# A decoder layer on one Trainium2 core: weights of the out and down projections are loaded from the inputs into plain tiles and split from there

## The chip, the core and the metric

The kernel runs on one core of a Trainium2 chip. A core has a matrix engine (PE, TensorE, with its weight loads shown apart as PEld), a vector engine (DVE), a scalar engine (ACT), a general engine (POOL), a queue engine (SP) and 16 DMA engines that move data between DRAM and the on-chip memory. Each engine executes its own list of instructions in order, and waits on semaphores for the others. DMAs are issued by SP (queue q1), ACT (q10) and POOL (q0), each in its own order too: a DMA whose condition isn't met holds up whatever stands behind it in its issuer's list.

The metric is the device time of one execution in microseconds (us), lower is better. PE, DVE, ACT and POOL below are the names of the profile.

## The reference

One layer of a hybrid decoder on x of 2048 tokens by 1024 channels, in float32:

```python
h = rmsnorm(x, norm1)
z = h @ w_in                      # q, k, v | conv a, gate | lru gate, x
y = concat(attention(q, k, v),    # dilated sliding windows, 6 heads
           conv_module(a, gate),  # causal depthwise conv of 31 taps, LayerNorm, swish
           gelu(lru_gate) * rg_lru(conv4(lru_x)))
x = x + y @ w_out                                      # 1024 x 1024
x = x + relu(rmsnorm(x, norm2) @ w_up)**2 @ w_down     # 1024 x 4096, 4096 x 1024
return rmsnorm(x, final)
```

## The kernel before

**Split products.** Every large product is made of float32 operands that are split into a high half (a rounded copy, made on ACT by a CAST) and a low half (the rest, made on DVE by a subtraction). `halves(raw, h, l)` does both (L925 and L926; the copy of it for the in-projection is L242 and L243). A product then takes three matmuls: high by high, high by low, low by high. Up and down are besides done by a scheme of seven products of half blocks in place of eight.

**Stages.** The 2048 tokens are worked on in two halves h of 1024. The in-projection of half 0 fills about 0 to 257 us of the profiled span, that of half 1 about 257 to 500. Beside the second, the mixers of half 0 (attention, conv, LRU) run on DVE, ACT and POOL, with some small matmuls on PE. Then, for each half, come the out-projection (`outproj`, sixteen steps n, each of 24 matmuls into one of four banks), up (`up`) and down (`down`, 56 steps); half 0 takes about 500 to 1269 us, half 1 the rest. The mixers of half 1 lie in pieces beside up and down of half 0.

**What sets the order.** A scheduler puts each engine's instructions in order from the written program, its priorities and its own estimate of times. `issue_after` holds an instruction behind another, `high_priority` moves a group forward, and `sp_order` keeps the order in which the loads of `outproj` and `up` are written.

**Out and down weights.** Right behind the in-projection of half 0, ACT issues two DMAs from DRAM to DRAM: `out_w` is a copy of all of `w_out` (L1608), `down_w` of the left halves of the first sixteen row tiles of `w_down` (L1609), 4 MB each. `out_load(w)` (L953) loads one 128 by 1024 tile of `out_w` into the low tile of that weight's pair, and `out_split(w)` splits it in place; for w of 2 and 3 the pair is made of tiles of X. In `down`, block t of the weights is loaded by `t_load(t)` and split by `t_split(t)`. The first eight blocks (product 1) come from `down_w` into their own low tile (L1315) and are split in place, the later ones through the tiles `kept` and `second`.

**LRU of half 0** (`lru_mixer`). For each of three channel tiles a load `wide<-lscr` (L550, 513.5 KB, issued by SP) brings the projected x; DVE makes the four conv taps (L557, then L561 three times); ACT and DVE split the result (`wr<-wide`); PE makes the gates (L573 to L575). In the same stage PE works through the in-projection of half 1 (L262, L265, L268), whose results DVE takes out of the banks (`z<-mm`, L390 to L395) with the factor `row` of the norm (ACT L361, DVE L362).

**Change of halves.** Near the end of down of half 0 (`hooks(kp)`, and the lines behind `tail = down(...)`), the first steps of the next out-projection are put in front of the last work of `down`. That last work (`finish`) stores the output rows: DVE L1439 scales them in place, POOL L1443 stores them (`out<-v`, `out<-z`). The tiles of `low1` (`low_tiles(1)`) lie where `z1`, the last of these output tiles, was.

Of the kernel before, what the change touches and what calls it, by code (L numbers as in the profile page):

```python
# [12 lines left out]
P = 128  # L13
# [66 lines left out]
def body(tc, xt, w_in, w_v, w_out, w_up, w_down, vecs, lru_wa, lru_wx, consts, g_row, out, out_rows):  # L80
# [96 lines left out]
    gates_w = tc.dram_tile([3, P, 4 * P], F32, name="gates_w")  # L177
    out_w = tc.dram_tile([KT, P, HS], F32, name="out_w")
    cscr = tc.dram_tile([P, HS], F32, name="cscr")
    down_w = tc.dram_tile([2 * KT, P, NB], F32, name="down_w")  # L180

# [769 lines left out]

    def out_load(w, pairs):
        nc.sync.dma_start(f32(out_pair(w, pairs)[1]), out_w[CHANNELS[w]])  # L953

    def out_split(w, pairs):
        wh, wl = out_pair(w, pairs)
        halves(f32(wl), wh, wl)

# [10 lines left out]

    def out_first(pairs):  # L970
        out_load(0, pairs)
        out_load(1, pairs)
# [8 lines left out]
    def out_second(h, pairs):  # L981
        if not h:
            out_load(2, pairs)
            out_load(3, pairs)
        for n0, n1 in ((0, 2), (2, 4), (4, 5), (5, 8)):
            act_load(h, 0, n0, n1)

    def low_tiles(h):
        lp = pool(f"low{h}", 1, side="right", reuse_waits="tile")
        wraw = lp.tile([P, 4 * NB], F32, name="wraw")  # L990
        more = [lp.tile([P, HS], F32R, name=f"pair{5 + i}") for i in range(3)]
        plain = lp.tile([P, 3 * NB], F32, name="low")
        rest = [lp.tile([P, NB], F32, name=f"low{i}") for i in range(13)]
        at = [wraw[:, i * NB:(i + 1) * NB] for i in range(4)] + [plain[:, i * NB:(i + 1) * NB] for i in range(3)] + rest
        return wraw, plain, at, more

# [53 lines left out]

    def outproj(h, wts, banks, begun):
        at, pairs = wts.at, wts.pairs
# [44 lines left out]
        if not begun:  # L1097
            out_second(h, pairs)
        in_order = sp_order()
        residual(0)  # L1100
        residual(1)
        for n in range(16):
            if n >= begun:
                out_matmuls(n, pairs, banks, range(4))
                tick(OUT_SHARE)
                out_matmuls(n, pairs, banks, range(4, KT))
            w = {0: 1, 1: 2, 2: 3, 4: 6, 5: 7, 6: 4, 7: 5}.get(n, 0)
            if w > begun:
                out_split(w, pairs)
            if 1 <= n < 4:  # L1110
                for i in range(*((0, 3), (3, 6), (6, 8))[n - 1]):
                    act_split(0, i)
            if n == 12:
                for k in (2, 3):
                    split_op(S1, k, tiles[k][S1])
            with first():
                nc.vector.tensor_add(e_at[n % es], e_at[n % es], banks[n % 4])
            if 2 <= n < 6:
                out_load((6, 7, 4, 5)[n - 2], pairs)
            evac(n)  # L1120
            if n + 2 < 16:
                residual(n + 2)
            if n == 10:
                wts.load(0)
            elif n == 13:
                wts.sums(0)
                wts.first()
            elif n == 14:
                wts.second()
                wts.load_plain(0)  # L1130
            in_order()
            tick(OUT_SHARE)
# [151 lines left out]

    def down_steps(h):
        kept, second = [], []

        def t_tiles(t):
# [17 lines left out]
        def t_load(t):  # L1306
# [24 lines left out]
        def t_split(t):  # L1331
            n, kp = divmod(t, 8)
            th, tl = t_tiles(t)
            halves(f32(tl) if n == 0 else second[t % 3] if PRODUCTS[n] == 3 else kept[kp], th, tl)

        return s_load, s_split, s_tiles, t_load, t_sum, t_split, t_tiles, kept, second

    def down_prologue(steps):
        s_load, s_split, s_tiles, t_load, t_sum, t_split = steps[:6]

        def stage(i):
            if i == 0:
                s_load(0)
                t_load(2)
            elif i == 1:
                t_load(3)
            elif i == 2:
                t_load(0)
                t_load(4)
            elif i == 3:  # L1350
                s_load(1)
                t_load(5)
                t_split(2)
            elif i == 4:
                t_load(1)
                t_split(3)
            else:
                s_load(2)
                s_load(3)
                s_split(0)  # L1360
                t_split(0)
                s_split(1)
                t_split(1)

        return stage

    def down(h, steps, banks, hooks):
# [125 lines left out]

        upto = {"s load": 4, "s split": 2, "load": 6, "sum": 6, "split": 4}

# [110 lines left out]
    inproj(0)  # L1606
    with tc.issue_after(next(i for i in reversed(nc.cur_bb.bb.instructions) if i.engine == mybir.EngineType.Activation)):
        nc.scalar.dma_start(out_w, w_out)  # L1608
        nc.scalar.dma_start(down_w, w_down[0:2 * KT, :, 0:NB])  # L1609
    with tc.issue_after(last_x[0].ins):  # L1610
# [10 lines left out]
    def between(n):  # L1621
# [3 lines left out]
        elif n == len(COLUMN_ORDER[1]) - 2:  # L1625
            close("wide")
            pairs.extend(left_pairs(0))
            out_first(pairs)

    inproj(1, between)  # L1630
    close("pmain", "z", "plain")
    aside[0] = mixers(1)
# [6 lines left out]
    for h in range(2):  # L1639
        wraw, plain, at, more = low_tiles(h)  # L1640
        pairs = pairs + more
        wts = Weights(wraw, plain, at, pairs)
        rest = outproj(h, wts, banks, begun)
        steps = down_steps(h)
        up(h, wts, banks, rest, down_prologue(steps))
# [4 lines left out]
        def hooks(kp):  # L1650
# [3 lines left out]
            elif h == 0 and kp == 1:  # L1654
# [3 lines left out]
                state_["pairs"] = left_pairs(1)  # L1658
            elif h == 0 and kp == 2:
                out_load(0, state_["pairs"])  # L1660
            elif h == 0:
                for n0, n1 in ((), ((0, 2),), ((2, 4),), ((4, 5), (5, 6)), ((6, 8),), ())[kp - 2]:
                    act_load(1, 1, n0, n1)
                if kp in (3, 5, 6):
                    out_load({3: 1, 5: 2, 6: 3}[kp], state_["pairs"])
                if kp > 3:
                    act_split(1, 2 * kp - 8)
                    act_split(1, 2 * kp - 7)
                if kp == 5:
                    out_split(0, state_["pairs"])  # L1670

        tail = down(h, steps, banks, hooks)
        close(f"second{h}")
        if h:
            while chores:
                chore()
            run(tail)
            close("early1", "late1")
        else:
            pairs = state_["pairs"]  # L1680
            out_matmuls(0, pairs, banks, range(KT))
            out_second(1, pairs)
            while chores:
# [6 lines left out]
            run(tail)  # L1690
            close("late0")
            begun = 2
# [45 lines left out]
```

## Time and profile before

| | before |
|---|---|
| median of 3 runs | 1989.8 us (1986.52 to 1991.84) |
| profiled execution, its own time | 1988.35 us |
| its span, first to last instruction | 1986.5 us |
| mean granted TensorE clock | 0.994 |
| DVE busy | 1448.0 us (73%) |
| ACT busy | 1054.4 us (53%) |
| POOL busy | 168.2 us (8%) |
| moved by DMA | 399.78 MB: q1 342.02, q0 45.38, q10 10.76 |
| DRAM read, written | 287.47 MB, 119.00 MB |

The same span by stage:

| stretch, us | PE busy | DVE busy | ACT busy | PE clock |
|---|---|---|---|---|
| 0 to 257 (257) | 245.81 | 225.99 | 146.53 | 1.00 |
| 257 to 500 (243) | 223.18 | 161.10 | 101.59 | 0.96 |
| 500 to 1269 (769) | 762.34 | 596.57 | 462.71 | 1.00 |
| 1269 to 1986.5 (717.5) | 707.36 | 464.30 | 343.56 | 1.00 |

What PE is not busy is the difference of the first number in a row's brackets and its PE time: 11.2, 19.8, 6.7 and 10.1 us. The last column is the clock that the throttle granted to PE, 1.00 being full speed; a busy PE at a low clock loses time that doesn't show as idle.

### The profile page before, as it was taken

Reading aid. Unit: us, or ns where it says so; the run is one execution under the profiler, and the core shown is the slowest. Engines: PE = TensorE matmul, PEld = TensorE weight load, DVE = VectorE, ACT = ScalarE, POOL = GpSimd, SP = SyncE. Lnnn points to the kernel's source line nnn. Section 1 sums busy time; section 2 is a strip of 40 time slices with the busy share of each in tenths; the row PEclk is TensorE's granted clock in tenths of the full one; section 3 lists DMA queues with packets and bytes.
Section 4 is the critical chain, followed back from the end, with each engine's and each line's share of the span. In section 5 each row is a group of like instructions: output and inputs, shape, how many; then the busy total and the mean of one; then the engine's idle time right before and its main releaser. Section 6 shows DMA issues by size and latency. Waiting matters only on the chain.

```text
span 1986.5 us, 25512 instructions
## 1 busy us (share of the span) xinstructions
PE 1938.7 (98%) x8906; PEld 1590.3 (80%) x8906; DVE 1448.0 (73%) x1976; ACT 1054.4 (53%) x1637; POOL 168.2 (8%) x297
## 2 busy tenths in 40 slices
PE   7999979999999999999999999999999999999998
PEld 6887757779787787888888888788888887888886
DVE  7899766784568665878878899867555555577884
ACT  6145946513558764555565566346555545444343
POOL 0024100000023413000000000100000000000001
PEclk9999989999999999999999999999999999999999
DMA  5556586635556647445788687764444447786773
GB/s 170 159 160 184 161 281 200 208 125 160 184 173 185 207 149 234 169 151 179 272 292 293 225 287 248 249 194 146 149 148 149 154 148 259 240 285 212 264 260 138
DMA packets 202124, 399.78 MB, mean 201 GB/s; under 512 B 25382, under 2 KB 33814, under 8 KB 201932
## 3 DMA queue, kind: packets, MB, share of 16 engines
q1 hardware_dynamic: 182548, 342.02, 51.2%
q0 software_dynamic: 16096, 45.38, 7.9%
q10 hardware_dynamic: 3352, 10.76, 1.6%
q8 instruction: 70, 1.15, 0.2%
q14 instruction: 58, 0.48, 0.1%
HBM read 287.47 MB, written 119.00 MB: 205 GB/s over the span
## 4 chain that ended last, share of the span: by engine, by line
PE 70%; DVE 12%; DMA 9%; ACT 5%; issue 4%; SPq 0%; POOL 0%; DVEq 0%; ACTq 0%; POOLq 0%
PE bank L1153 9%; PE bank L1154 9%; PE bank L1155 9%; PE bank L1517 7%; PE bank L1515 7%; PE bank L1516 7%; PE mm L262 3%; PE mm L268 3%; PE mm L265 3%; PE bank L966 2%; PE bank L967 2%; PE bank L968 2%; DVE wide L474 2%; DMA second<-in_w_down 2%; DVE rounded L926 1%
## 5 line engine op out<-in xcount | busy, mean ns | idle before, releaser
L1153 PE MATMUL bank<-rounded,pair 128*128 128x512 f32 x896 | 351.2, 392 | 2.7 <-ACT low L1162 2.0
L1154 PE MATMUL bank<-rounded,pair 128*128 128x512 f32 x896 | 351.0, 392 | 0.0
L1155 PE MATMUL bank<-rounded,pair 128*128 128x512 f32 x896 | 350.9, 392 | 0.0
L1515 PE MATMUL bank<-rounded,rounded 128*128 128x512 f32 x688 | 268.1, 390 | 1.6 <-DVE z L1528 0.8
L1517 PE MATMUL bank<-rounded,rounded 128*128 128x512 f32 x688 | 268.0, 389 | 1.4 <-DVE rounded L926 1.4
L1516 PE MATMUL bank<-rounded,rounded 128*128 128x512 f32 x688 | 267.7, 389 | 0.0
L926 DVE TENSOR_TENSOR rounded<-rounded 128x1024 fp32r<-128x1024 f32 (+1 forms) x172 | 186.9, 1098 | 73.0 <-ACT rounded L925 72.6
L925 ACT CAST rounded<-rounded 128x1024 fp32r<-128x1024 f32 (+1 forms) x172 | 161.1, 949 | 132.2 <-DMA rounded<-fscr 92.1
L1153 PEld LDWEIGHTS bank<-rounded,pair 128*128 128x128 f32 x896 | 168.4, 188 | 40.1 <-ACT low L1162 2.4
L1155 PEld LDWEIGHTS bank<-rounded,pair 128*128 128x128 f32 x896 | 168.2, 188 | 36.0 <-issue 0.2
L1154 PEld LDWEIGHTS bank<-rounded,pair 128*128 128x128 f32 x896 | 168.2, 188 | 35.4 <-issue 0.2
L262 PE MATMUL mm<-rounded,rounded 128*128 128x512 f32 x496 | 159.7, 398 | 8.5 <-ACT rounded L242 6.6
L265 PE MATMUL mm<-rounded,rounded 128*128 128x512 f32 x496 | 158.6, 396 | 0.0
L268 PE MATMUL mm<-rounded,rounded 128*128 128x512 f32 x496 | 157.8, 395 | 0.0
L925 ACT CAST rounded<-kept 128x1024 fp32r<-128x1024 f32 x80 | 84.0, 1050 | 136.8 <-DVE kept L1325 67.0
L1515 PEld LDWEIGHTS bank<-rounded,rounded 128*128 128x128 f32 x688 | 129.1, 188 | 29.5 <-DVE z L1528 1.3
L1517 PEld LDWEIGHTS bank<-rounded,rounded 128*128 128x128 f32 x688 | 129.2, 188 | 29.1 <-DVE rounded L926 2.3
L1516 PEld LDWEIGHTS bank<-rounded,rounded 128*128 128x128 f32 x688 | 129.2, 188 | 27.0
L242 ACT CAST rounded<-raw 128x512 fp32r<-128x512 f32 (+1 forms) x96 | 55.7, 583 | 145.1 <-PE mm L265 91.1
L925 ACT CAST pair<-wraw 128x1024 fp32r<-128x1024 f32 x64 | 67.1, 1048 | 112.6 <-PE bank L1154 108.3
L926 DVE TENSOR_TENSOR rounded<-kept,rounded 128x1024 fp32r<-128x1024 f32 x80 | 97.8, 1223 | 38.4 <-ACT rounded L925 38.1
L926 DVE TENSOR_TENSOR pair<-wraw,pair 128x1024 fp32r<-128x1024 f32 x64 | 78.2, 1222 | 61.6 <-ACT pair L925 61.5
(375 smaller groups left out, 3680.3 us busy)
## 6 DMA issues: line engine op xcount, KB each, us to landing
fscr<-low SPq DMA_DIRECT2D x224, 256.0 KB, 2.1
rounded<-fscr SPq DMA_DIRECT2D x112, 512.0 KB, 3.9
second<-in_w_down SPq DMA_DIRECT2D x80, 512.0 KB, 5.4
kept<-in_w_down SPq DMA_DIRECT2D x48, 512.0 KB, 5.3
raw<-in_w_in SPq DMA_DIRECT2D x64, 256.0 KB, 3.9
low<-in_w_up SPq DMA_DIRECT2D x64, 256.0 KB, 3.1
wraw<-in_w_up SPq DMA_DIRECT2D x64, 256.0 KB, 2.9
raw<-in_xt SPq DMA_DIRECT2D x32, 256.0 KB, 3.4
```

Source lines behind the costliest of these rows:

```text
L242: nc.scalar.copy(h, raw)
L262: nc.tensor.matmul(bank, wh[:, sl], ah[:, cols], start=first_, stop=False)
L265: nc.tensor.matmul(bank, wh[:, sl], al[:, cols], start=False, stop=False)
L268: nc.tensor.matmul(bank, wl[:, sl], ah[:, cols], start=False, stop=last_)
L925: nc.scalar.copy(h, raw)
L926: nc.vector.tensor_sub(l, raw, f32(h))
L1153: nc.tensor.matmul(bank, wh[:, sl], hi(x), start=fresh and k == 0, stop=False, **kw)
L1154: nc.tensor.matmul(bank, wh[:, sl], lo(x), start=False, stop=False, **kw)
L1155: nc.tensor.matmul(bank, wl[:, sl], hi(x), start=False, stop=k == KH - 1, **kw)
L1515: nc.tensor.matmul(banks[j], th[:, c], sh[:, x], start=fresh and k0, stop=False, **kw)
L1516: nc.tensor.matmul(banks[j], th[:, c], sl[:, x], start=False, stop=False, **kw)
L1517: nc.tensor.matmul(banks[j], tl[:, c], sh[:, x], start=False, stop=k1, **kw)
```

## The change

The two DRAM copies and their tensors are gone. `out_load(w, tile_)` loads from `w_out` into a plain tile that it is given, and `out_split` splits from that tile into the pair. `t_load` loads the blocks of product 1 from `w_down`, the first six into three `two` tiles, the others into `second`. The lines that are left out give the plain tiles: a new pool `stage` of two tiles for w of 0 and 1 in half 0, and in `low_tiles` five tiles `two` of twice the width in place of ten single ones.

```diff
-    out_w = tc.dram_tile([KT, P, HS], F32, name="out_w")
-    down_w = tc.dram_tile([2 * KT, P, NB], F32, name="down_w")
...
-    def out_load(w, pairs):
-        nc.sync.dma_start(f32(out_pair(w, pairs)[1]), out_w[CHANNELS[w]])
+    plain_w = {}
+
+    def out_load(w, tile_):
+        plain_w[w] = tile_
+        nc.sync.dma_start(tile_, w_out[CHANNELS[w]])
 
     def out_split(w, pairs):
         wh, wl = out_pair(w, pairs)
-        halves(f32(wl), wh, wl)
+        halves(plain_w.pop(w), wh, wl)
...
         if not begun:
-            out_second(h, pairs)
+            out_second(h, twos)
+        else:
+            out_load(3, twos[1])
...
             if 2 <= n < 6:
-                out_load((6, 7, 4, 5)[n - 2], pairs)
+                out_load((6, 7, 4, 5)[n - 2], twos[n % 2])
...
+        plain_t = {t: twos[i] for t, i in ((2, 0), (3, 1), (0, 2), (4, 0), (5, 1), (1, 2))}
...
             if i == 1:
-                nc.sync.dma_start(two(f32(t_tiles(t)[1])), down_w[2 * kp:2 * kp + 2].rearrange("k p n -> p k n"))
+                block(plain_t[t] if t in plain_t else second[t % 3], 0, 0)
...
-        upto = {"s load": 4, "s split": 2, "load": 6, "sum": 6, "split": 4}
+        upto = {"s load": 4, "s split": 2, "load": 6, "sum": 6, "split": 6}
...
-    with tc.issue_after(next(i for i in reversed(nc.cur_bb.bb.instructions) if i.engine == mybir.EngineType.Activation)):
-        nc.scalar.dma_start(out_w, w_out)
-        nc.scalar.dma_start(down_w, w_down[0:2 * KT, :, 0:NB])
...
-            elif h == 0 and kp == 2:
-                out_load(0, state_["pairs"])
...
-                if kp in (3, 5, 6):
-                    out_load({3: 1, 5: 2, 6: 3}[kp], state_["pairs"])
...
+                for n0, n1 in {6: ((2, 4),), 7: ((4, 5), (5, 8))}.get(kp, ()):
+                    act_load(1, 0, n0, n1)
+                if 3 <= kp < 6:
+                    out_load(kp - 3, steps[8][(kp - 1) % 3])
...
-            out_second(1, pairs)
+            act_load(1, 0, 0, 2)
```

For half 1 the loads of w of 0, 1 and 2 go into the tiles `second` at kp of 3, 4 and 5, and that of w of 3 is written at the head of `outproj(1)`, into `two1`. In the prologue of down, each of the first six blocks is loaded a stage earlier and all six are split there, where before it was four.

The scheduler then moves other work as well. **The first LRU tile of half 0.** These are ACT's rows of before behind the in-projection of half 0; DMAs in ACT's list are issued there, and `x2` marks two like rows:

```order
L404 ACTIVATE z<-z 128x1024 [waits DVE_49]
L1608 DMA out_w<-in_w_out 64x16384 [waits DMAHW4_49]
L1609 DMA down_w<-in_w_down 2048x512 [waits DMAHW6_49]
L361 ACT_TABLE_LOAD
L361 ACTIVATE row_105<-mm,eps_r 128x512 [waits PE_49] x2
```

After the change the same place of ACT's list reads (line numbers are two lower here):

```order
L402 ACTIVATE z<-z 128x1024 [waits DVE_49]
L502 ACT_TABLE_LOAD
L502 ACTIVATE wide<-cb,eps_l 128x512 [waits PE_49]
L240 CAST rounded_83<-raw_99 128x512 [waits DMAHW3_49,PE_49,Activation_49]
L781 COPY m<-mb 128x128
```

The copies are gone, and a square root of the conv mixer (L502, L504 of before) stands ahead of the factor of the norm. On DVE this is what stood between the statistics of the attention (L755, L760) and the taps of the LRU (L557, which waits for the load `wide<-lscr`):

```order
L755 ISA m,stat_142<-mb,m 128x128 [waits PE_49]
L760 TENSOR_SCALAR ncol_144<-stat_142 128x2 [waits DVE_49]
L557 TENSOR_SCALAR wide<-wide,vec 128x1024 [waits DMAHW3_49]
L561 SCALAR_TENSOR_TENSOR wide<-wide,vec 128x1024 [waits DVE_49] x3
L362 RECIPROCAL row_105<-row_105 128x512 [waits Activation_49] x2
L393 TENSOR_TENSOR z<-mm,row_105 128x512 [waits DVE_49,PE_49] x2
```

And this is what stands there now (the taps are L555 and L559):

```order
L758 TENSOR_SCALAR ncol_142<-stat_140 128x2 [waits DVE_49]
L503 RECIPROCAL wide<-wide 128x512 [waits Activation_49]
L241 TENSOR_TENSOR rounded_83<-raw_99,rounded_83 128x512 [waits DMAHW3_49,PE_49,Activation_49]
L753 ISA m,stat_140<-mb,m 128x128 [waits PE_49]
L506 TENSOR_TENSOR wide<-wide 128x512 [waits DVE_49]
L555 TENSOR_SCALAR wide<-wide,vec 128x1024 [waits DMAHW3_49]
L559 SCALAR_TENSOR_TENSOR wide<-wide,vec 128x1024 [waits DVE_49] x3
L360 RECIPROCAL row_105<-row_105 128x512 [waits Activation_49] x2
L391 TENSOR_TENSOR z<-mm,row_105 128x512 [waits DVE_49,PE_49] x2
```

Work of the conv and the attention now precedes the taps in DVE's list.

**The change of halves.** SP's rows of before, at the first steps of `outproj(1)`; `m<-in_xt` loads the residual, `xscr` and `ascr` are scratch, `pair_9839` and `pair_9841` are the low tiles of w of 6 and 7:

```order
L1066 DMA m<-in_xt 128x512 [waits DMAHW0_49,DMASW7_49]
L1066 DMA m<-in_xt 128x512 [waits DMASW7_49,DMAHW1_49,DMASW6_49,DMASW2_49]
L1074 DMA xscr<-m 128x512 [waits DMAHW2_49,DVE_49]
L1066 DMA m<-in_xt 128x512 [waits DMAHW3_49,DMASW7_49]
L1074 DMA xscr<-m 128x512 [waits DMAHW4_49,DVE_49]
L1081 DMA ascr<-wraw 128x512 [waits DMAHW5_49,Activation_49]
L1066 DMA m<-in_xt 128x512 [waits DMAHW6_49]
L953 DMA pair_9839<-out_w 128x1024 [waits DMAHW7_49]
```

SP's rows now, from the same residual on; the first `two_9840` is w of 3, `two_9839` is w of 6, and DMASW1 to DMASW4 are semaphores of stores that POOL issues:

```order
L1069 DMA m<-in_xt 128x512 [waits DMAHW5_49,DMASW7_49]
L1069 DMA m<-in_xt 128x512 [waits DMASW7_49,DMAHW6_49,DMASW6_49,DMASW2_49]
L1077 DMA xscr<-m 128x512 [waits DMAHW7_49,DVE_49]
L1069 DMA m<-in_xt 128x512 [waits DMAHW0_49,DMASW7_49]
L1077 DMA xscr<-m 128x512 [waits DMAHW1_49,DVE_49]
L954 DMA two_9840<-in_w_out 128x1024 [waits DMASW3_49,DMASW4_49,DMASW2_49,DMAHW2_49,DMASW1_49,DVE_49]
L1084 DMA ascr<-wraw 128x512 [waits DMAHW3_49,Activation_49]
L1069 DMA m<-in_xt 128x512 [waits DMAHW4_49]
L954 DMA two_9839<-in_w_out 128x1024 [waits DMAHW5_49]
```

The load of w of 3 now stands here, and waits for the last four stores of `z1`, over which `two1` lies. On PE, before, the second step that uses `rounded7` (the pair of w of 2 and 3; bank 4011) followed right upon the first (bank 4014):

```order
L967 MATMUL bank_4014<-rounded_80,rounded_9486 128x512
L968 MATMUL bank_4014<-rounded_80,rounded_9486 128x512
L966 MATMUL bank_4011<-rounded_79,rounded_9486 128x512
L967 MATMUL bank_4011<-rounded_79,rounded_9486 128x512
L968 MATMUL bank_4011<-rounded_79,rounded_9486 128x512
```

Now a whole step on `pair0` (bank 4016, 24 matmuls) and nine matmuls of the next (bank 4017) lie between; its last rows, and the first of the second `rounded7` step (bank 4015):

```order
L969 MATMUL bank_4016<-rounded_82,pair_9488 128x512
L967 MATMUL bank_4017<-rounded_81,pair_9489 128x512 [waits DVE_49]
L968 MATMUL bank_4017<-rounded_81,pair_9489 128x512
L969 MATMUL bank_4017<-rounded_81,pair_9490 128x512
L967 MATMUL bank_4015<-rounded_79,rounded_9483 128x512 [waits Activation_49]
L968 MATMUL bank_4015<-rounded_79,rounded_9483 128x512
```

The wait for ACT in that row is for the CAST of w of 3 from `two1`.

More of the change, by code (lines that the diff above doesn't have):

```diff
@@ L968, in out_matmuls, with out_first @@
             nc.tensor.matmul(bank, wl[:, sl], hi(b0 + k), start=False, stop=k == KT - 1)
-    def out_first(pairs):
-        out_load(0, pairs)
-        out_load(1, pairs)
+    def out_first(pairs, tiles):
+        out_load(0, tiles[0])
+        out_load(1, tiles[1])
         for n0, n1 in ((0, 2), (2, 4), (4, 5), (5, 8)):
@@ L979, in out_first, with out_second @@
                 act_split(1, n)
[L981 to L984, printed above, removed]
+            out_split(1, pairs)
+    def out_second(h, tiles):
+        out_load(2, tiles[0])
+        out_load(3, tiles[1])
         for n0, n1 in ((0, 2), (2, 4), (4, 5), (5, 8)):
@@ L992, in low_tiles @@
         plain = lp.tile([P, 3 * NB], F32, name="low")
-        rest = [lp.tile([P, NB], F32, name=f"low{i}") for i in range(13)]
-        at = [wraw[:, i * NB:(i + 1) * NB] for i in range(4)] + [plain[:, i * NB:(i + 1) * NB] for i in range(3)] + rest
-        return wraw, plain, at, more
+        twos = [lp.tile([P, HS], F32, name=f"two{i}") for i in range(5)]
+        ones = [lp.tile([P, NB], F32, name=f"low{i}") for i in range(3)]
+        both = [t[:, i * NB:(i + 1) * NB] for t in twos for i in range(2)]
+        at = [wraw[:, i * NB:(i + 1) * NB] for i in range(4)] + [plain[:, i * NB:(i + 1) * NB] for i in range(3)]
+        return wraw, plain, at + ones[:1] + both[:4] + ones[1:] + both[4:], more, twos
     class Weights:
@@ L1049, in sp_order, with outproj @@
         return in_order
-    def outproj(h, wts, banks, begun):
+    def outproj(h, wts, banks, begun, twos):
         at, pairs = wts.at, wts.pairs
@@ L1106, in outproj @@
                 out_matmuls(n, pairs, banks, range(4, KT))
-            w = {0: 1, 1: 2, 2: 3, 4: 6, 5: 7, 6: 4, 7: 5}.get(n, 0)
-            if w > begun:
+            w = {1: 2, 2: 3, 4: 6, 5: 7, 6: 4, 7: 5}.get(n)
+            if w in plain_w:
                 out_split(w, pairs)
@@ L1283, in up, with down_steps @@
             done = (a21, a22, a11, a12)
-    def down_steps(h):
+    def down_steps(h, twos):
         kept, second = [], []
+        plain_t = {t: twos[i] for t, i in ((2, 0), (3, 1), (0, 2), (4, 0), (5, 1), (1, 2))}
         def t_tiles(t):
@@ L1333, in t_split @@
             th, tl = t_tiles(t)
-            halves(f32(tl) if n == 0 else second[t % 3] if PRODUCTS[n] == 3 else kept[kp], th, tl)
+            halves(plain_t[t] if t in plain_t else second[t % 3] if n == 0 or PRODUCTS[n] == 3 else kept[kp], th, tl)
         return s_load, s_split, s_tiles, t_load, t_sum, t_split, t_tiles, kept, second
@@ L1344, in stage @@
                 t_load(2)
+                t_load(3)
             elif i == 1:
-                t_load(3)
+                t_load(0)
             elif i == 2:
-                t_load(0)
+                t_split(2)
                 t_load(4)
@@ L1351, in stage @@
                 s_load(1)
+                t_split(3)
                 t_load(5)
-                t_split(2)
             elif i == 4:
+                t_split(0)
                 t_load(1)
-                t_split(3)
+                t_split(4)
             else:
@@ L1360, in stage @@
                 s_split(0)
-                t_split(0)
                 s_split(1)
                 t_split(1)
+                t_split(5)
         return stage
@@ L1627, in between @@
             pairs.extend(left_pairs(0))
-            out_first(pairs)
+            stage = pool("stage", 1, reuse_waits="tile")
+            out_first(pairs, [stage.tile([P, HS], F32, name=f"stage{i}") for i in range(2)])
     inproj(1, between)
-    close("pmain", "z", "plain")
+    close("pmain", "z", "plain", "stage")
     aside[0] = mixers(1)
@@ L1639, in body @@
     for h in range(2):
-        wraw, plain, at, more = low_tiles(h)
+        wraw, plain, at, more, twos = low_tiles(h)
         pairs = pairs + more
         wts = Weights(wraw, plain, at, pairs)
-        rest = outproj(h, wts, banks, begun)
-        steps = down_steps(h)
+        rest = outproj(h, wts, banks, begun, twos)
+        steps = down_steps(h, twos[2:])
         up(h, wts, banks, rest, down_prologue(steps))
@@ L1670, in hooks @@
                     out_split(0, state_["pairs"])
+                for n0, n1 in {6: ((2, 4),), 7: ((4, 5), (5, 8))}.get(kp, ()):
+                    act_load(1, 0, n0, n1)
+                if 3 <= kp < 6:
+                    out_load(kp - 3, steps[8][(kp - 1) % 3])
         tail = down(h, steps, banks, hooks)
-        close(f"second{h}")
         if h:
@@ L1677, in body @@
             run(tail)
-            close("early1", "late1")
+            close("second1", "early1", "late1")
         else:
@@ L1690, in body @@
             run(tail)
-            close("late0")
+            close("second0", "late0")
             begun = 2
```

## The prediction

> **What bounds the kernel now.** I start with the page: busy time of the engines, then the forty slices of the span (49.7 us each).
>
> ```profile
> PE 1938.7 (98%) x8906; PEld 1590.3 (80%) x8906; DVE 1448.0 (73%) x1976; ACT 1054.4 (53%) x1637; POOL 168.2 (8%) x297
> ...
> PE   7999979999999999999999999999999999999998
> ...
> PEclk9999989999999999999999999999999999999999
> DMA  5556586635556647445788687764444447786773
> ```
>
> PE is busy for 1938.7 of 1986.5 us, so all idle time of PE together is 47.8 us, and no rearrangement of loads can win more than that and what a low clock costs. Three slices show idle time: the start, the end, and slice 6 (248 to 298 us). Slice 6 is also the one with a low clock and the one of the busiest DMA engines in the first half of the span. The change removes two DMAs that are issued just there, so the next view is the table by windows, with the waits of 255 to 345 us (columns: total, times, longest).
>
> ```profile
> 250.00:300.00 50.00, 35.59 (x145) 27.26 (x144) 30.65 (x42) 21.97 (x38) 0.00 (x0) 0.85 0.86 281
> 300.00:350.00 50.00, 48.80 (x214) 38.81 (x212) 31.03 (x52) 32.62 (x43) 1.79 (x3) 0.98 0.65 199
> ...
> DVE wide L557 <- DMA wide<-lscr: 22.5, 2, 18.3
> ...
> PE cb L573 <- ACT wr L242: 10.1, 1, 10.1
> ACT wr L242 <- DVE wide L561: 10.0, 2, 9.8
> ...
> PE mb L753 <- DVE stat L755: 3.3, 1, 3.3
> ```
>
> PE lacks 50 - 35.59 = 14.4 us in the first window and 1.2 in the second. Read from the bottom up the waits are one chain: PE waits 10.1 us for the split of the LRU input, ACT waits for the taps, DVE waits 18.3 us for the load `wide<-lscr`. The timeline (start, duration, engine, and idle time before it in brackets) and the chain of waits give the times:
>
> ```profile
> 258.73 0.63 ACTq L1608 DMA_DIRECT2D out_w<-in_w_out  x1
> 260.40 0.50 ACTq L1609 DMA_DIRECT2D down_w<-in_w_down  x1
> ...
> 260.31 0.42 SPq L550 DMA_DIRECT2D wide<-lscr  x1
> ...
> 281.80 0.81 DVE L557 TENSOR_SCALAR wide<-wide,vec 128x1024 f32<-128x1024 f32 x1 [18.30 <-DMA wide<-lscr]
> ...
> 287.33 0.80 PE L573 MATMUL cb<-wr 128*128 128x512 f32 x1 [10.05 <-ACT wr L242]
> ...
> 296.25 0.80 PE L753 MATMUL mb<-mr 128*128 128x256 f32 x2 [3.28 <-DVE stat L755]
> ```
>
> ```profile
> 260.31 21.47 DMA wide<-lscr
> ...
> 323.19 4.39 DMA wide<-lscr
> ```
>
> The copies are issued at 258.7 and 260.4; the load that is issued beside them takes 21.5 us, the same load at 323.2 takes 4.4. That is the contention: 17 us of delay on DVE, which executes in order and so can't do the reciprocals (L362) and the evacuations behind it either. PE runs dry twice, for 10.05 and for 3.28 us. Behind both the clock is low:
>
> ```profile
> 285.00:290.00 5.00, 2.67 (x6) 2.15 (x7) 4.96 (x4) 1.18 (x2) 0.00 (x0) 0.50 1.04 329
> 290.00:295.00 5.00, 2.97 (x10) 2.01 (x8) 5.00 (x5) 2.13 (x3) 0.00 (x0) 0.84 0.27 102
> 295.00:300.00 5.00, 3.75 (x11) 3.17 (x12) 5.00 (x8) 0.71 (x3) 0.00 (x0) 0.50 0.70 221
> 300.00:305.00 5.00, 5.00 (x20) 4.05 (x19) 2.46 (x5) 2.44 (x3) 0.00 (x0) 0.83 0.02 4
> ```
>
> Busy time by what the clock lacks: 2.67 x 0.50 + 2.97 x 0.16 = 1.8 us behind the first wait, 3.75 x 0.50 + 5.00 x 0.17 = 2.7 behind the second.
>
> [...]
>
> **First term: the stall at 260 to 302 us.** It costs 14.4 + 1.2 us idle and 1.8 + 2.7 us of low clock, 20.1 together. Not all of it goes. In the new order ACT makes the root of the conv mixer ahead of the factor of the norm (`row`), each with a table load of its own, and PE's next matmuls use the bank that the factor is read from.
>
> ```profile
> 272.70 1.28 ACT L766 ACT_TABLE_LOAD   x1
> ```
>
> I replayed the new order of PE, ACT and DVE by hand with the durations of the trace. PE then waits 2.2 us near 273 for the factor (two table loads of 1.28 us, less what lies beside other work), and up to 1 us at each of two later gates of the LRU; there is no wait at the first. The 1.2 us of the second window I leave in. 20.1 - 2.2 - 2 - 1.2 = **14.7 us gained**. The bounds: at least the wait of 10.05 us and the clock behind it without those 2.2 (10.05 + 1.8 - 2.2 = 9.6), at most all but the 1.2 (18.9). From 302 us on PE is nearly always busy, so what is won there is kept unless something else ends last; the next such place is at 430 to 450 us:
>
> ```profile
> 430.00:450.00 20.00, 17.45 (x80) 15.55 (x79) 13.46 (x16) 3.68 (x7) 0.00 (x0) 0.91 0.52 176
> ...
> PE mm L425 <- DVE z L393: 2.5, 1, 2.5
> ```
>
> There PE lacks 2.55 us and about 17.45 x 0.09 = 1.6 us of clock, by an evacuation that stands late in DVE's list. DVE arrives earlier and has fewer taps ahead of it now; I take **1 us gained**, between -1 (the order gets a little worse) and 4.1 (all of it).
>
> **Second term: the change of halves.** The load of w of 3 now waits for the last stores of `z1`, in SP's list, and PE has 24 + 9 matmuls to do before it needs the result. The rows of before at this place, from the timeline of POOL, ACT, SP and DVE, a window of 2 us, and one piece of the chain of waits:
>
> ```profile
> 1285.54 2.14 POOL L1443 DMA_DIRECT2D out<-z  x4
> ...
> 1297.02 0.72 ACT L1073 ACTIVATE low<-m,vec 128x512 f32<-128x512 f32 x1 [4.54 <-DMA out<-z]
> ...
> 1285.52 0.87 SPq L953 DMA_DIRECT2D pair<-out_w  x1
> ...
> 1289.91 0.66 SPq L953 DMA_DIRECT2D pair<-out_w  x1
> ...
> 1287.24 0.69 DVE L1117 TENSOR_TENSOR m<-m,bank 128x512 f32<-128x512 f32 x1 [0.40 <-PE bank L968]
> ...
> 1291.00:1293.00 2.00, 2.00 (x11) 1.65 (x10) 0.49 (x1) 0.64 (x1) 0.00 (x0) 1.00 1.03 415
> ...
> 1276.31 0.23 PE bank L966
> ```
>
> The median landing times of like DMAs, from the table of DMA issues (the last number), and the cast and the subtraction of such a tile (mean ns of one behind the bar):
>
> ```profile
> out<-z POOLq DMA_DIRECT2D x20, 256.0 KB, 6.4
> ...
> out<-v POOLq DMA_DIRECT2D x4, 256.0 KB, 2.8
> ...
> second<-in_w_down SPq DMA_DIRECT2D x80, 512.0 KB, 5.4
> ...
> rounded<-down_w SPq DMA_DIRECT2D x16, 512.0 KB, 5.8
> ...
> rounded<-fscr SPq DMA_DIRECT2D x112, 512.0 KB, 3.9
> ...
> L925 ACT CAST rounded<-kept 128x1024 fp32r<-128x1024 f32 x80 | 84.0, 1050 | 136.8 <-DVE kept L1325 67.0
> ...
> L926 DVE TENSOR_TENSOR rounded<-kept,rounded 128x1024 fp32r<-128x1024 f32 x80 | 97.8, 1223 | 38.4 <-ACT rounded L925 38.1
> ```
>
> PE ends the step before at about 1287.1 (DVE takes its bank at 1287.24). 33 matmuls of 0.23 us cover it to 1294.7. The last of the four stores is issued at about 1287.15. In before they had landed by 1297.0, while two loads of 512 KB ran beside them and the DMA engines were full (share 1.03). Of these two loads the first is now the one that waits, so I take the stores' median, 6.4 us: landed at 1293.5. The load, 5.4 us, ends at 1298.9, the cast, 1.05 us, at 1300.0. PE waits 5.3 us, and loses some 2.5 us of clock behind it (1.8 and 2.7 above): **7.8 us lost**. The bounds: stores in 2.8 us and load in 3.9 give 1295.0, a wait of 0.3 and no loss to speak of; stores at 1297.0 as before and load in 5.8 give 1303.9, a wait of 9.2 and 2.7 of clock, 11.9 lost. Behind the waiting load on SP stand `ascr`, the residual `m` and the load of w of 6. They are needed one step later or more (the residual by an evacuation whose bank comes up again only after three further steps, 3 x 24 x 0.23 = 16.6 us), so they cost nothing as long as the wait stays under some 12 us. The weights of 6, 7, 4 and 5 then pass through two tiles by turns: per tile 5.4 + 1.05 us and a subtraction of 1.22, against 11 us of matmuls (48 x 0.23) for each weight.
>
> **The rest at nothing.** As many splits, and loads of the same size; the 8 MB that the copies read and wrote are gone. Two casts and two subtractions of down's prologue come earlier. The waits there that they could lengthen or shorten are small:
>
> ```profile
> PE bank L1517 <- DVE rounded L926: 1.4, 2, 0.9
> ```
>
> I bound this at 2 us either way; if ACT and DVE had no idle time in the prologue, the four would cost 2 x 1.05 + 2 x 1.2 = 4.5 us once per half.
>
> **Sum.** Profiled execution 1988.35 - 14.7 - 1 + 7.8 = **1980.5 us**. The median of the runs is 1.45 us above the profiled one, 1989.8, so this is 0.4 to 0.5% faster. About 0.3%, or 6 us, is what a measurement of this kernel can tell from no change: faster is below 1983.8, slower above 1995.8.
>
> [...]
>
> **The rivals.**
> 1. *The stores are early.* The full DMA engines of before were due to the loads beside the stores, and one of them now waits. Then the wait of PE is 0 to 1 us: 1988.35 - 14.7 - 1 + 0.5 = 1973. For it: share 1.03 at 1291; against it: the stores' median is 6.4 us over all twenty.
> 2. *The stores are as late as before.* 11.9 us lost: 1988.35 - 14.7 - 1 + 11.9 = 1984.6; with the smallest first term, 9.6, it is 1989.7, no change. For it: ACT really waited until 1297.02.
> 3. *The first stall only changes its name (slower).* In DVE's new list, statistics, a reciprocal and multiplies of conv and attention stand ahead of the taps, each waiting for PE or ACT. If one of them holds DVE until about 281.8, as the load did, the first term is 0 and only the second is left: 1988.35 + 7.8 = 1996.2. It decides for slower when less than about 0.5 us of the first term is won. Against it: ACT and PE have their inputs by 276 in the replay, and `wide<-lscr` at 4.4 us would land at 265.
> 4. *The copies weren't the cause*, and the load takes its 21.5 us from traffic of its own queue; the change then doesn't do what it says in this stage. The time is that of 3, but the wait would still read `wide<-lscr`. The 4.4 us of the second load speak against it.
>
> **How the numbers follow.** Forecast (1977 to 1985) 0.45; stores early (below 1977) 0.25; stores late (1985 to 1991) 0.18; 3 and 4 together 0.12, a third of it with enough of the first term left to be no change. Faster by over 0.3%: most of the forecast and all of the first rival, 0.67; within 0.3%: the end of the forecast, the second rival and that third, 0.24; slower 0.09. The likeliest case gives the time, 1980.5. The range leaves out the best ends of both terms and the slower cases: 1970 to 1990.
>
> **What would show it.** In the profile after: slice 6 of PE at 9 with PEclk 9; `wide<-lscr` near 4 to 5 us and no long wait at the taps; PE's wait for the gates gone. A new wait of PE near 1280 us on ACT's cast `rounded<-two`, 5 us long, with SP waiting for `out<-z` at the load of w of 3, and a clock of about 0.5 for some 5 us behind it. PE idle outside these two places within 2 us of before. Wrong would be: DVE waiting 10 us or more ahead of the taps (rival 3), a load of over 15 us there (rival 4), or PE's idle time growing in down or up, which no term here covers.

## The result: 1.0% faster, and outside the predicted range

| | before | after |
|---|---|---|
| median | 1988.63 us (4 runs, 1986.52 to 1991.84) | 1967.61 us (4 runs, 1966.72 to 1970.98) |
| ratio of after to before | | 0.9896, 95% interval 0.9877 to 0.9915 |
| profiled execution, its own time | 1988.35 us | 1968.2 us |
| its span | 1986.5 us | 1966.4 us |

1980.5 was forecast, with a range of 1970 to 1990. The direction was right; the gain, 20 us, is two and a half times the 8 that were forecast.

**The profile after.** The page's busy times and slices (a slice is 49.2 us here):

```profile
PE 1933.0 (98%) x8906; PEld 1585.9 (81%) x8906; DVE 1448.0 (74%) x1976; ACT 1050.9 (53%) x1635; POOL 168.4 (9%) x297
...
PE   8999999999999999999999999999999999999998
...
PEclk9999999999999999999999999999999999999999
DMA  5556557444666657445787696755444436686773
```

Slice 6 of PE has gone from 7 to 9, and its clock from 8 to 9. PE's idle time fell from 47.8 to 1966.4 - 1933.0 = 33.4 us, by 14.4. The same 8906 matmuls kept PE busy 1938.7 us before and 1933.0 now: those 5.7 us were low clock. Together this is the 20.1 us of the spans.

Where they were won, the same stretches of the program show, in before and in after. A stretch begins or ends with a certain matmul: the first of the out-projection of half 0 (508.1 and 487.8 us), the last gate of the LRU (1202.5, 1180.8), the last `pair` step of the out-projection of half 1 (1357.4, 1338.7), the last of down's product with two `rounded` tiles (1928.9, 1908.3). Columns: stretch, its length, busy times, clock, DMA share, GB/s. Before:

```profile
257.00:508.10 251.10, 231.28 (x1034) 191.57 (x1034) 165.61 (x214) 104.31 (x146) 8.70 (x15) 0.96 0.59 190
508.10:1202.50 694.40, 688.04 (x3218) 560.64 (x3218) 534.73 (x769) 421.55 (x659) 95.42 (x165) 1.00 0.66 218
1202.50:1357.40 154.90, 153.98 (x675) 126.03 (x674) 121.33 (x155) 79.31 (x114) 9.94 (x18) 1.00 0.65 212
1357.40:1928.90 571.50, 569.77 (x2502) 469.09 (x2501) 369.60 (x402) 281.78 (x377) 0.00 (x0) 1.00 0.58 203
```

After:

```profile
257.00:487.80 230.80, 224.84 (x1036) 186.63 (x1035) 165.92 (x216) 101.80 (x145) 8.72 (x15) 1.00 0.54 169
487.80:1180.80 693.00, 688.74 (x3218) 561.79 (x3218) 535.70 (x770) 421.01 (x658) 95.51 (x165) 1.00 0.66 219
1180.80:1338.70 157.90, 155.04 (x675) 125.79 (x674) 121.83 (x155) 80.74 (x116) 9.94 (x18) 1.00 0.64 208
1338.70:1908.30 569.60, 569.35 (x2501) 468.99 (x2500) 369.26 (x402) 281.58 (x377) 0.00 (x0) 1.00 0.59 204
```

The stage of the mixers is 251.1 - 230.8 = 20.3 us shorter (13.9 idle, 6.4 busy at a higher clock). Up and down of half 0 win 1.4, the change of halves loses 3.0, half 1 wins 1.9, and the rest, 57.6 against 58.1 us, loses 0.5: 20.1.

**The stage of the mixers after**, by windows, by waits and by the DMA issues of 257 to 282 us:

```profile
250.00:300.00 50.00, 46.81 (x216) 36.34 (x215) 40.09 (x66) 41.05 (x65) 0.60 (x1) 1.00 0.64 194
300.00:350.00 50.00, 47.23 (x201) 36.76 (x200) 39.29 (x48) 28.86 (x35) 3.08 (x6) 1.00 0.73 233
...
430.00:450.00 20.00, 20.00 (x117) 19.98 (x116) 7.31 (x14) 5.25 (x10) 4.83 (x8) 1.00 0.66 183
```

```profile
DVE wide L555 <- DMA wide<-lscr: 2.7, 2, 1.6
...
PE mm L260 <- ACT row L359: 2.3, 1, 2.3
...
PE cb L571 <- ACT wr L240: 1.3, 1, 1.3
```

```profile
wide<-lscr SPq DMA_DIRECT2D x1, 513.5 KB, 6.2
```

The load takes 6.2 us in place of 21.5, DVE's wait for it is at most 1.6 in place of 18.3, and PE's wait for the first gate is gone. PE's wait of 2.3 us for the factor of the norm stands where the replay had 2.2. What is idle there, 3.2 + 2.8 us, is close to the 5.4 that the prediction left in. The stall at 430 to 450 us has gone altogether.

**The change of halves after**, by the timelines of DVE, POOL, SP, ACT and PE:

```profile
1265.37 0.69 DVE L1122 TENSOR_TENSOR m<-m,bank 128x512 f32<-128x512 f32 x1 [0.42 <-PE bank L969]
...
1263.65 2.21 POOL L1451 DMA_DIRECT2D out<-z  x4
...
1269.46 0.33 SPq L954 DMA_DIRECT2D two<-in_w_out  x1
...
1269.43 0.72 ACT L1076 ACTIVATE low<-m,vec 128x512 f32<-128x512 f32 x1 [2.97 <-DMA out<-z]
...
1274.00 1.04 ACT L923 CAST rounded<-two 128x1024 fp32r<-128x1024 f32 x1 [3.34 <-DMA two<-in_w_out]
...
1275.10 0.50 PE L967 MATMUL bank<-rounded,rounded 128*128 128x512 f32 x1 [2.28 <-ACT rounded L923]
```

The chain is the one that was forecast: stores, load, cast, matmul. PE came to the place at 1275.10 - 2.28 = 1272.8, which is 1265.2 and 33 matmuls of 0.23 us. But the last store was issued at about 1265.3 and all had landed by 1269.4, 4.1 us later and not 6.4; the load was in by 1274.0, 4.5 us and not 5.4. While these stores were under way SP issued nothing (1261.3 to 1269.5 us), where before it issued six DMAs at 1284.3 to 1289.9; that this made the stores faster is read from the traces and wasn't tried apart. So PE waits 2.3 us, and its clock stays at 1.00 behind it.

### The profile page after: what moved, and what is told of

It is laid out like the page before. It is cut to its first block, busy times and chain, and to the rows that moved or that the text cites. A ratio compares the mean times of both kernels' runs of the same rounds, so it can differ in the third digit from the quotient of the medians.

```text
span 1966.4 us, 25491 instructions
## 1 busy us (share of the span) xinstructions
PE 1933.0 (98%) x8906; PEld 1585.9 (81%) x8906; DVE 1448.0 (74%) x1976; ACT 1050.9 (53%) x1635; POOL 168.4 (9%) x297
## 4 chain that ended last, share of the span: by engine, by line
PE 82%; DMA 6%; DVE 6%; ACT 3%; issue 2%; POOL 0%; SPq 0%; DVEq 0%; ACTq 0%; POOLq 0%
PE bank L1158 10%; PE bank L1159 10%; PE bank L1160 10%; PE bank L1523 9%; PE bank L1525 9%; PE bank L1524 9%; PE mm L260 4%; PE mm L263 4%; PE mm L266 4%; PE bank L969 2%; PE bank L967 2%; PE bank L968 2%; DMA raw<-in_xt 1%; PE mm L423 1%; PE mm L425 1%
## 5 line engine op out<-in xcount | busy, mean ns | idle before, releaser
L924 DVE TENSOR_TENSOR rounded<-rounded 128x1024 fp32r<-128x1024 f32 (+1 forms) x152 | 162.4, 1080 | 62.5 <-ACT rounded L923 62.1
L923 ACT CAST rounded<-rounded 128x1024 fp32r<-128x1024 f32 (+1 forms) x152 | 139.9, 935 | 112.4 <-DMA rounded<-fscr 89.0
L260 PE MATMUL mm<-rounded,rounded 128*128 128x512 f32 x496 | 158.3, 395 | 10.4 <-ACT rounded L240 7.0
L266 PE MATMUL mm<-rounded,rounded 128*128 128x512 f32 x496 | 156.4, 392 | 0.0
L263 PE MATMUL mm<-rounded,rounded 128*128 128x512 f32 x496 | 156.3, 393 | 0.0
```

What stands on the lines that cost most here:

```text
L260: nc.tensor.matmul(bank, wh[:, sl], ah[:, cols], start=first_, stop=False)
L263: nc.tensor.matmul(bank, wh[:, sl], al[:, cols], start=False, stop=False)
L266: nc.tensor.matmul(bank, wl[:, sl], ah[:, cols], start=False, stop=last_)
L923: nc.scalar.copy(h, raw)
L924: nc.vector.tensor_sub(l, raw, f32(h))
```

## The experiments

All ratios are to runs of the kernel before on the same chip, taken beside them. "Load" is the first `wide<-lscr`; "start" is the time of the first matmul of the out-projection of half 0 in the profiled execution. That one execution can lie off the median: by 7.6 us in out_rows, 3.7 in down_only, 3.0 in before_rows (all slower than their medians), and at most 2.1 in the others of this table.

| kernel | copies | load, us | start, us | median, us | ratio, 95% interval |
|---|---|---|---|---|---|
| before | 4 MB in 64 KB pieces, 4 MB in 2 KB | 21.5 | 508.1 | 1988.63 | 1 |
| after | none | 6.2 | 487.8 | 1967.61 | 0.9896 (0.9877 to 0.9915) |
| both_copies | as before, unused | 21.0 | 505.2 | 1987.16 | 0.9995 (0.9977 to 1.0012) |
| half_copies | 4 MB in 64 KB pieces | 18.4 | 506.1 | 1985.39 | 0.9979 (0.9956 to 1.0003) |
| out_rows | 4 MB in 4 KB pieces | 13.0 | 500.8 | 1977.70 | 0.9946 (0.9930 to 0.9961) |
| down_only | 4 MB in 2 KB pieces | 10.5 | 500.5 | 1981.94 | 0.9966 (0.9948 to 0.9985) |
| before_rows | 4 MB in 4 KB pieces, 4 MB in 2 KB | 12.2 | 501.9 | 1983.67 | 0.9976 (0.9964 to 0.9989) |
| sliver | 0.5 MB in 32 KB pieces | 6.4 | 492.4 | 1970.40 | 0.9915 (0.9890 to 0.9939) |

**The copies put back, without use (both_copies).**

```diff
...
     inproj(0)
+    with tc.issue_after(next(i for i in reversed(nc.cur_bb.bb.instructions) if i.engine == mybir.EngineType.Activation)):
+        nc.scalar.dma_start(out_w, w_out)
+        nc.scalar.dma_start(down_w, w_down[0:2 * KT, :, 0:NB])
```

> The changed kernel with the two DRAM copies put back where they were (nothing reads them); weights still come straight from the inputs. With a DMA issued at that place the scheduler falls back to the order of before for the mixers of half 0. Theory A (the traffic of the copies is the cause): the load of the LRU input takes about 21 us again, PE lacks some 14 us at 260 to 300 us, and the time is 1987 to 1990 us. Theory B (the new data path of the weights, fewer or earlier loads, won the time): the time stays at 1968 to 1971.

All of the gain is gone: 1987.16 us, not to be told from before. The load takes 21.0 us, and PE lacks 13.5 us at 250 to 300 us:

```profile
250.00:300.00 50.00, 36.54 (x147) 28.29 (x146) 30.08 (x40) 21.20 (x36) 0.00 (x0) 0.86 0.83 277
```

The new data path of the weights by itself, with its changed loads, tiles and splits, wins nothing that can be measured (the interval leaves it 0.23% at most). Theory B falls.

**A sixteenth of the bytes, in the same order (sliver).** With a DMA at that place, here of 0.5 MB, the scheduler chooses the order of before for the mixers; this run has that order and hardly any traffic. The traces of both_copies, sliver, half_copies, out_rows and down_only list the same instructions in the same order on every engine, so these five differ in their copies alone. The edit, against both_copies:

```diff
-        nc.scalar.dma_start(out_w, w_out)
-        nc.scalar.dma_start(down_w, w_down[0:2 * KT, :, 0:NB])
+        nc.scalar.dma_start(out_w[0:1], w_out[0:1])
```

> As the one with both copies, but only a sixteenth of their bytes is copied (512 KB of 8 MB), at the same place. The orders of PE, DVE and SP are those of the kernel with both copies. Theory A1 (traffic alone): the load of the LRU input takes 4 to 7 us, and the time is 1968 to 1971. Theory A2 (the order of the mixers that comes with a DMA at this place, not the bytes): 1985 to 1990. Between them, the part above 1968 is what the order costs.

1970.40 us: the copying is the cause, and the order is the smaller part. The starts divide it: 505.2 - 492.4 = 12.8 us by the traffic, 492.4 - 487.8 = 4.6 by the order (the sliver's own 0.5 MB among it). Each start is of one execution; the 2.9 us between both_copies and before, which have the same copies and the same order at this place, show how far two such can lie apart. By the medians the parts are 16.8 and 2.8 us, and the intervals of sliver and after overlap. Where the order costs, sliver's window and wait show:

```profile
400.00:430.00 30.00, 26.14 (x110) 22.17 (x109) 25.62 (x28) 4.97 (x8) 0.00 (x0) 0.89 0.38 128
...
PE mm L425 <- DVE z L393: 3.9, 1, 3.9
```

It is the late evacuation that stood at 430 to 450 us in before. It doesn't need the bytes of the copies; it comes with the order of before, and in after it is absent.

**Half of the copies (half_copies).**

```diff
         nc.scalar.dma_start(out_w, w_out)
-        nc.scalar.dma_start(down_w, w_down[0:2 * KT, :, 0:NB])
```

> As the one with both copies, but only the copy of the out weights (4 MB). Theory A1: the load of the LRU input ends when this copy does, some 10 us after it was issued in place of 21.5, so half of the delay, and the time is 1973 to 1979. Theory A2: as with both copies, 1985 to 1990.

The time, 1985.39 us, is that of A2, but sliver, with the same order, rules A2 out. A1's time is missed: half of the bytes did not cost half, the load still takes 18.4 us. What A1 said of the end holds, though: the copy lands at 276.9 us and the load 2.5 us behind it, at 279.4. A1 had the copy at some 10 us, and it takes 17.5:

```profile
out_w<-in_w_out ACTq DMA_DIRECT2D x1, 17.5
```

The DMA rows of 261 to 280 us (packets, MB, share), while that load was under way, suggested that the load has to wait for the copy because of its pieces:

```profile
q10 hardware_dynamic: 75, 3.87, 60.9%
q1 hardware_dynamic: 589, 1.60, 25.3%
```

The copy's 3.87 MB are 59 pieces of 64 KB (the other 16 records have 4 bytes each); the 589 of SP's queue have 2.7 KB on average.

**The same 4 MB in smaller pieces (out_rows, down_only, before_rows).** The first pads the rows of `out_w` by 64 bytes, so that no piece is longer than a row; the second copies only the down weights, which were in 2 KB pieces all along; the third is the kernel before with padded rows. The edit of the first, against half_copies:

```diff
-    out_w = tc.dram_tile([KT, P, HS], F32, name="out_w")
+    out_w = tc.dram_tile([KT, P, HS + 16], F32, name="out_w")
...
-        nc.scalar.dma_start(out_w, w_out)
+        nc.scalar.dma_start(out_w[:, :, :HS], w_out)
```

> As the kernel with only the copy of the out weights (4 MB), in the same order on every engine, but the copy goes to rows that are padded by 64 bytes, so that it moves in pieces of 4 KB in place of 64 KB. Theory P (what delays the load of the LRU input is the size of the copy's pieces, which pass ahead of the load's own 4 KB pieces one for one): that load takes 6 to 10 us in place of 18.4, and the time is 1970 to 1976 us. Theory B (the bytes of the copy): the load takes about 18 us again, and the time is 1983 to 1988.

> The changed kernel with only the copy of the down weights put back (4 MB, in pieces of 2 KB as before), in the order of the kernel with only the out copy. Theory P: the load of the LRU input takes 6 to 10 us, and the time is 1970 to 1976. Theory B: about 18 us and 1983 to 1988, as with the 4 MB of the out copy.

> The kernel before, with both copies, in its own order on every engine; only the rows of the out copy are padded by 64 bytes (pieces of 4 KB). Theory P: the load of the LRU input takes 8 to 14 us, and most of the stall goes without the new data path: 1972 to 1980. Theory B: 21 us and no change, 1986 to 1990.

The load falls to 13.0, 10.5 and 12.2 us. With 8 MB in small pieces it is faster than with 4 MB in large ones (12.2 against 18.4), so with these copies of 4 and 8 MB the size of the pieces counted for more than the bytes, as theory P has it, though the loads stay longer than the 6 to 10 us that it gave for 4 MB. The load no longer waits for the copy's end: in out_rows it lands at 274.1 us and the copy at 280.7. There the rows of 261 to 274 us read:

```profile
q10 hardware_dynamic: 628, 2.57, 59.6%
q1 hardware_dynamic: 640, 1.79, 39.7%
```

Packet for packet the two queues are now level, and SP's queue has 1.79 of 4.36 MB, 41%, in place of 1.60 of 5.47, 29%. The copy isn't slower here than in half_copies (2.57 MB in 13 us against 3.87 in 19, about 200 GB/s both); SP's queue is faster, 138 GB/s in place of 84. Theory P has the pieces pass one for one: out_rows' 628 and 640 records are nearly so, half_copies' 59 against 589 are not. How the large pieces hold up the load was not shown. The times are 1977.70, 1981.94 and 1983.67 us, and theory P's 1970 to 1976 and 1972 to 1980 are missed. In the profiled executions, which were slower than these medians, the taps start at 273 to 274 us, 8 earlier than before, but PE then waits for the statistics of the attention, which stand behind the reciprocals in DVE's list: 5.2 us in out_rows and before_rows and 4.2 in down_only, where before had 3.3.

**Copies elsewhere (late_a, late_b, early).** The kernel before with its own data path and both copies, issued later in the mixers (304 and 317 us in the profiles) or in the middle of the first in-projection (131 us). The edit, with n of 5, of 6, and in the other in-projection of 8:

```diff
+        if n == 5:
+            with tc.issue_after(next(i for i in reversed(nc.cur_bb.bb.instructions) if i.engine == mybir.EngineType.Activation)):
+                nc.scalar.dma_start(out_w, w_out)
+                nc.scalar.dma_start(down_w, w_down[0:2 * KT, :, 0:NB])
```

> The kernel before, with both copies and its own data path; only the two copies are issued later, behind the conv mixer's and the attention's first work of half 0 (by the new kernel's profile at about 295 us). Up to them every engine has the order of the changed kernel. Theory A (it is a load on which DVE waits at once that the copies must not meet): the first load of the LRU input takes 6 to 8 us, the stall at 260 to 300 us is gone, and what the copies now meet (the later LRU loads and the loads of the in-projection, which have slack) costs 0 to 8 us: 1968 to 1976. Theory E (wherever they are put, some 20 us of full DMA engines cost their 10 to 15 us in this stage): 1980 to 1988, with a new wait on a load of 10 us or more between 295 and 345 us.

> As the run before it, with the two copies one column of the in-projection later (about 305 us). Theory A: 1968 to 1976, within 3 us of the run before it. Theory E: 1980 to 1988.

> The kernel before, with both copies and its own data path; only the two copies are issued in the middle of the in-projection of half 0, some 100 us or more ahead of the mixers. Theory E1 (the copies cost so much because DVE and PE wait for loads at once in the mixers; in the in-projection the loads run ahead): the lost time there is below 6 us, the stretch from 257 us to the out-projection is as short as in the changed kernel within 6 us, and the time is 1968 to 1978 us. Theory E2 (anywhere some 20 us of full DMA engines cost 10 to 20 us): 1982 to 1992, with PE lacking 10 us or more ahead of 257 us.

The times of theory A and theory E1 are missed. late_a took 1993.06 us (ratio 1.0019, 1.0006 to 1.0031), late_b 1998.07 (1.0038, 1.0021 to 1.0054), early 1985.46 (0.9976, 0.9964 to 0.9988). PE lost a wait of 9 to 17 us in each. But none of these waits is the slow load of before, and they don't show what the traffic alone would cost there.

In late_a and late_b the first load takes 5.9 and 5.7 us, and the stall at 260 to 300 us is gone, as theory A has it. What is late then are the issues. In late_a SP issues nothing from 309.2 to 321.2 us; its next DMA waits for the semaphore that the first copy raises, and the copy lands at 320.8. ACT stands still before the issue of the second copy, with its casts behind it:

```profile
321.20 0.32 SPq L861 DMA_DIRECT2D m<-oscr  x1
...
331.95 0.50 ACTq L1622 DMA_DIRECT2D down_w<-in_w_down  x1
332.55 2.18 ACT L242 CAST rounded<-raw 128x512 fp32r<-128x512 f32 x4 [24.87 <-DMA m<-wscr]
```

In late_b ACT stands still for 22.3 us at the same place. A later load of the LRU input is late as well, for which DVE waits 24.4 us, but it is issued only at 361.4 us and takes 8.5 (window; then waits of 270 to 400 us, and SP's row):

```profile
350.00:400.00 50.00, 32.88 (x135) 26.09 (x134) 23.99 (x26) 21.46 (x24) 3.29 (x6) 0.83 0.63 212
...
DVE wide L557 <- DMA wide<-lscr: 26.1, 2, 24.4
...
PE cb L573 <- ACT wr L242: 18.4, 2, 17.1
...
361.40 0.33 SPq L550 DMA_DIRECT2D wide<-lscr  x1
```

In early PE waits 17.2 us in the first in-projection, for a split of the conv. It doesn't wait for a load: DVE, which makes the input of the split, is busy throughout (window, DVE's row, PE's wait). With the copies at this place the scheduler gives another order, and it put 24 taps of the conv behind each other with only evacuations between, where in before the attention's work stands between them too.

```profile
160.00:170.00 10.00, 0.00 (x0) 0.00 (x0) 10.00 (x10) 0.00 (x0) 0.00 (x0) 0.50 0.66 249
...
156.64 15.62 DVE L474 SCALAR_TENSOR_TENSOR wide<-wide,vec 128x1024 f32<-128x1024 f32 x13
...
PE cb L282 <- ACT wr L242: 17.2, 1, 17.2
```

Even so early is a little faster than before, and from the first matmul of the second in-projection (286.0 us) to the start of the out-projection (503.7) it takes 217.6 us, where after takes 222.5 and before 244.1. So the mixers there are as fast as theory E1 has them. Whether copies at this early place, with the order of before, would be free was not tried and stays open. Of the versions that ran, those that issue no copy are the fastest.

**The wait at the change of halves (w3_early, w3_behind).** The load of w of 3 in down of half 0 and its split right behind w of 2; then the same with both halves of the split held behind the last work of down.

```diff
-        else:
-            out_load(3, twos[1])
...
+                if kp == 7:
+                    out_load(3, steps[8][2])
...
             out_split(2, pairs)
+            out_split(3, pairs)
```

> The changed kernel with the load of w of 3 for half 1 issued in down of half 0, into a tile of second, and split right behind w of 2, so that nothing waits for the stores of z1. Theory C (the wait of 2.3 us of PE at the change of halves is the price of the new place of this load): that wait goes, and the time is 1964.5 to 1966. Rival D (the earlier split crowds DVE and ACT before the change of halves, where they have little idle time): 1967 to 1970, with a new wait of PE for the split of w of 1 or 2.

> The changed kernel with the load of w of 3 for half 1 in down of half 0, as in the earlier run, but its cast and subtraction held behind the last work of down on ACT and DVE. Theory C (the wait of 2.3 us for that load and the wait of 2.6 us that the early split made are both avoidable): neither shows, and the time is 1963.5 to 1966. Rival D (another split or evacuation becomes the late one there): a new wait of 2 us or more of PE between 1250 and 1300 us, 1967 to 1969.

Neither can be told from after: 1968.47 us (0.9904, 0.9880 to 0.9928) and 1968.18 (0.9904, 0.9889 to 0.9919). The wait for `two` is gone in both, and rival D holds by its times, though in w3_early the new wait isn't for a split of w of 1 or 2. It stands a few us ahead of the place, on the mean of the output rows:

```profile
1250.00:1260.00 10.00, 6.75 (x22) 4.85 (x21) 9.78 (x11) 3.76 (x8) 0.00 (x0) 0.83 0.00 1
...
1253.23 0.50 PE L284 MATMUL cb<-mr,ones_cr 128*128 128x512 f32 x1 [2.60 <-ACT mr L923]
```

DVE is busy for 9.78 of these 10 us, and the subtraction of w of 3, 1.2 us, stands ahead of the sum that the mean needs. In w3_behind that subtraction stands behind, but the wait for the mean is 2.1 us all the same; there ACT waited 5.3 us for the loads of the mixers' results (waits of 1240 to 1262 us):

```profile
ACT rounded L923 <- DMA rounded<-mscr: 5.3, 2, 3.2
...
PE cb L284 <- ACT mr L923: 2.1, 1, 2.1
```

The load of w of 3 is queued among these on SP in this kernel. That it delays them is read from the trace and wasn't tried apart. No version of these runs beats after.

## Why the prediction was wrong

**The cause of the first stall: right.** Beside the copies the load took 21.5 us (6.2 after), DVE waited at most 18.3 us for it (1.6), ACT 9.8 for DVE, PE 10.1 for ACT (at most 1.3), and the clock of 250 to 300 us was 0.85 (1.00). both_copies and sliver show the copying to be it. Rival 3 (a new wait ahead of the taps) and rival 4 (not the copies) didn't come.

**The first term: right in its mechanism, too small.** The sum had 14.7 us for the stretch to about 350 us and 1 for the stall at 430 to 450; measured are 20.3. Up to 350 us it was foreseen well: 6.0 us stayed idle against 5.4, so 15.6 - 6.0 idle and 4.5 of clock were won, 14.1 us. The step that failed is "I take 1 us gained" for what lies behind, which came to 6.2: all of that stall went (2.55 us idle and 1.6 of clock), and 2.0 us of idle time at 350 to 400, which no term had. The step supposed that DVE's earlier arrival would shorten the stall a little. In sliver DVE's taps start at 267 us, 15 earlier than before, and the late evacuation still costs PE 3.9 us of waiting at a clock of 0.89; it goes only with the new order. The 2.0 us at 350 to 400 went with the copies (sliver lacks 0.5 there). The prediction priced the new order at 270 us, but didn't replay it on to 450 us.

**The second term: right in its mechanism, too large.** 7.8 us were forecast and 3.0 measured for the stretch, 2.3 of them the wait. The cover (33 matmuls) was right to the tenth. The step that failed here is the two landing times, medians over the whole kernel (6.4 and 5.4 us), where the place itself gave 4.1 and 4.5, and with them the 2.5 us of clock, which a wait of 2.28 us didn't bring. This is the direction of rival 1, to which the prediction gave 0.25: the stores land earlier, probably because the loads beside them now wait. Its wait of 0 to 1 us was too short, for the load itself still takes 4.5.

**The rest at nothing: a little outside its 2 us.** Up and down of half 0 win 1.4 us, half 1 wins 1.9 and the end loses 0.5, 2.8 together. No experiment was made on it, and its cause stays open; behind the start sliver, both_copies and half_copies take 1476.5, 1478.1 and 1479.5 us with the same instructions in the same order, so 2.8 us between two single executions may be chance. (In the prologue of down only blocks 3 and 0 are loaded a stage earlier than before, not each of the first six.)

**The sum.** 15.7 - 7.8 was forecast, 20.3 - 3.0 + 2.8 came out. The three errors have one sign, so the time fell 2.4 us below the range, whose lower end had left out the best cases of both terms together.

## What to carry to other kernels

A large copy in the background was not free where an engine waits for a load at once: look at the load that is issued beside it, and compare how long the same load takes elsewhere (21.5 and 4.4 us here). In these runs its delay went with the size of the copy's pieces more than with its bytes, in the copies of 4 and 8 MB: 18.4 us beside 4 MB in large pieces, 12.2 beside 8 MB in small ones. Moving the copy is not a clean test: at other places it held up the engines that issue DMAs (ACT for 24.9 us in late_a), or came with another order. Where a change gives the scheduler another order, follow that order to the next stage in which an engine is late, since a second stall may vanish or come by it.

## What the runs showed of the hardware that was not expected

Half of the copied bytes gave almost the whole delay (18.4 against 21.0 us), and the same bytes in pieces of 4 KB in place of 64 KB gave 13.0.

The clock fell behind some of the short waits and not behind others. In up of half 0 of after, a wait of 2.5 us stands with a clock of 0.83 in the window in which it ended, 750 to 760 us, and the 2.6 us of w3_early with 0.83 at 1250 to 1260. before's wait of 2.0 us at the same matmuls left it at 1.00 (last row, 1.8 us behind that wait), as after's 2.28 us at 1273 did (1.00 at 1270 to 1285):

```profile
740.00:750.00 10.00, 8.77 (x39) 6.84 (x37) 7.26 (x10) 1.54 (x2) 3.77 (x7) 1.00 0.77 213
750.00:760.00 10.00, 8.75 (x31) 7.05 (x32) 3.96 (x6) 5.62 (x10) 0.00 (x0) 0.83 0.69 265
...
PE bank L1158 <- ACT two L1167: 2.5, 1, 2.5
...
775.00:780.00 5.00, 5.00 (x23) 4.10 (x23) 1.14 (x2) 3.48 (x6) 0.00 (x0) 1.00 0.92 357
```
